# Forgetting attention on one Trainium2 core: unstacked queries and keys, scores as three 64-row products per head, query blocks taken in pairs, probabilities written over their biases

## The chip, the cores and the metric

The kernel runs as one launch on one core of one Trainium2 chip (trn2). The metric is device time in microseconds (us). Lower is better. Of the kernel before there are three runs: 1128.99, 1127.75 and 1128.63 us, median 1128.63 us.

## What is computed

The reference is a two-layer decoder trunk over 512 tokens of width 1024 in float32. Layer 0 is dilated window attention followed by a gated convolutional feed-forward block (FFN). Then keys, values and forget gates are projected once, and layer 1 attends to them with 16 heads of 64 features and runs its own FFN. The change touches only layer 1's attention and the projections that feed it:

```python
def fox_mixer(xn, w_q, w_o, k, v, c):          # c: cumulative log forget gates
    q = (xn @ w_q).reshape(B, T, 16, 64)
    for i in range(T // 128):                   # query blocks of 128
        s = einsum(q[block i], k[:, :q1]) * 64 ** -0.5
        s = s + (c[queries] - c[keys])          # per head
        s = where(causal, s, -1e30)
        p = softmax(s)
        out_i = einsum(p, v[:, :q1])            # keys up to the block's end only
    return concatenate(outs) @ w_o
```

Block i sees (i + 1) * 128 keys, so the four blocks of a head are unequal: 128, 256, 384 and 512 keys.

## The kernel before

**Precision.** The matrix products of the projections and the scores run in the type fp32r, which keeps fewer bits than float32. So every operand is split into a high part (a cast to fp32r) and a low part (value minus high part), and a product becomes three: high times high, high times low, low times high (`mm3`, lines 262 to 265).

**Stages and order.** The kernel has a hand-written order (`manual_schedule`): each engine executes its instructions in the order in which the program issues them, and semaphores hold an instruction back until its operands and its destination buffer are ready. All PSUM tiles come from one pool of 8 banks (`bank`), and the pools of SBUF tiles are `t8` (16 tiles), `t4` (10 tiles) and `t2` (8 tiles). A new tile takes a buffer that an older tile has left, and its first writer waits for that tile's last reader. After layer 0's FFN come the key projections (`keys`, lines 1294 to 1305), the value projections, and the attention loop (lines 1571 to 1607), then the output projection (`po`) and layer 1's FFN.

**Stacked keys and queries.** A head has 64 features, half of the 128 rows of TensorE's array. The kernel stacks the parts: for a head, the key tile `kst` holds the high part in the head's own 64 partitions and the low part in the other 64. The query tile `qst` holds two arrangements, high over low and, swapped, low over high. One product of 128 rows over the first arrangement gives high*high + low*low, and one over the second the two mixed terms, so a head's scores take two products (lines 1493 to 1497). The stacking costs two half-height casts on ScalarE and two half-height subtractions on VectorE for each pair of heads, for keys (1302, 1305) and for queries (`q_high` 1415, `q_low` 1423). The swapped query arrangement is made by two SBUF-to-SBUF DMAs of the GpSimd queue (1425, 1426).

**The loop.** `j` counts 8 pairs of heads, `i` 4 query blocks; a unit is one (j, i) with both heads, 32 units in all. In pass n the program issues, for unit n: `f_scores` (4 products of 128 rows, over at least 256 key columns), the normalisation of unit n-1 (`f_norm`: a reciprocal and two scalings on VectorE), `f_exp` (per head: VectorE adds the bias to the scores in PSUM and takes the row minimum of the negated sum, line 1506; ScalarE takes the exponential with the row sum, 1508), the bias of unit n+1 on GpSimd (`f_bias`, lines 1475 to 1483), a quarter of a later query projection (`q_part`, 6 products of 512 columns), then the transposes of the probabilities of unit n-2 (`f_transpose` on TensorE, 1530, with ScalarE copies out of PSUM, 1532). In every second pass come the products with the values of two older units (`f_pv`, 1545: 64-column products, one head in each half of the array's columns). Around the units, ScalarE and a GpSimd DMA that adds in flight split the weights of a later query projection (`W.high(minus=True)`, lines 54 and 56; `W.low_added`, line 77), SP loads the gates' rows (`load_ck`, 1391) and raw weights, and the finished output is split (`f_out_high` 1555, `f_out_low` 1559). In the last 8 passes the first quarter-products of the output projection (`po.both`) fill in where no query projection is left.

## Time and profile before

| | |
|---|---|
| median of the three runs | 1128.63 us (1127.75 to 1128.99) |
| span of the profiled execution, first to last instruction | 1125.8 us |
| what lies around the span, against the median | 2.83 us |
| TensorE (PE) busy in the span | 1114.3 us, 99% |
| granted TensorE clock, mean | 0.999 of full speed |
| attention loop, first score product to first product of the rest of the output projection | 631.75 to 742.34 us |

The profile gives no other time of the profiled execution than its span, so steps are counted against the span, and 2.83 us are added to compare with runs. A matrix product has two records: its weight load (PEld) and the product (PE). A product's record is longer than the time it holds the array: it includes its way through the array, so the records of consecutive products overlap, and the pace is read from start to start. A tile size like 64*128 in a row is rows by columns of the array that the product uses. A product of float32 operands (not fp32r) appears as two records.

### The profile page before, as it was taken

The page shows a single profiled execution, that of the slowest core. Times are in us where ns is not written, and L with a number is a line of the kernel's source. Part 1 is how long each engine was busy: PE and PEld are TensorE (multiplying, and loading weights), DVE is VectorE, ACT ScalarE, POOL GpSimd, SP SyncE. Part 2 cuts the span into 40 slices and gives each one's busy share as a digit, 9 for nine tenths or more (in the row PEclk, how much of TensorE's full clock was granted, in tenths as well). Part 3 has the DMA queues.
Part 4 walks back from the last instruction along what each step waited for, and adds up shares of the span by engine and source line. Part 5 has one row for each costly group of instructions (what it writes and reads, how often), then busy time and mean ns, then how long its engine had stood idle before and what let it go on. Part 6 is the DMA issues. An engine that isn't in the chain of part 4 may idle for free. (4 is left out here: it accounts for less than half of the span.)

```text
span 1125.8 us, 17268 instructions
## 1 busy us (share of the span) xinstructions
PE 1114.3 (99%) x6267; PEld 950.6 (84%) x6267; DVE 893.8 (79%) x1449; ACT 616.5 (55%) x1038; POOL 191.6 (17%) x291
## 2 busy tenths in 40 slices
PE   9999999999999999999999999999999999999997
PEld 6988889889899888888778888789989989988886
DVE  6668778888888689997588677847888788689894
ACT  5454565545444456576562588746444454456572
POOL 1832101200000121000000556600400000121000
PEclk9999999999999999999999999999999999999999
DMA  9469854333443699793447766473334343499861
GB/s 322 150 222 407 320 161 133 94 119 106 142 123 115 160 346 370 293 333 100 128 151 253 235 168 160 123 209 107 118 94 122 115 138 122 138 351 368 326 243 75
DMA packets 179471, 218.38 MB, mean 194 GB/s; under 512 B 11257, under 2 KB 131049, under 8 KB 179386
## 3 DMA queue, kind: packets, MB, share of 16 engines
q1 hardware_dynamic: 168634, 180.84, 49.0%
q0 software_dynamic: 10752, 36.45, 10.5%
q8 instruction: 49, 0.80, 0.3%
q14 instruction: 36, 0.29, 0.1%
HBM read 166.08 MB, written 39.63 MB: 183 GB/s over the span
## 5 line engine op out<-in xcount | busy, mean ns | idle before, releaser
L592 ACT ACTIVATE bb<-up,conv 128x512 f32<-128x512 f32 x80 | 60.6, 775 | 149.5 <-DVE up L917 76.2
L62 DVE TENSOR_TENSOR w<-wraw,w 128x1024 fp32r<-128x1024 f32 x96 | 123.0, 1312 | 22.1 <-ACT w L54 21.6
L54 ACT CAST w<-wraw 128x1024 fp32r<-128x1024 f32 x110 | 111.6, 1047 | 19.4 <-PE v_ps L264 11.6
L263 PE MATMUL acc<-w 128*128 128x512 f32 (+1 forms) x311 | 120.7, 388 | 1.1 <-DVE mix L310 1.1
L265 PE MATMUL acc<-w 128*128 128x512 f32 (+1 forms) x311 | 120.6, 388 | 0.0
L263 PE MATMUL up<-xch,w 128*128 128x512 f32 (+1 forms) x292 | 104.9, 359 | 0.0
L264 PE MATMUL up<-xcl,w 128*128 128x512 f32 (+1 forms) x292 | 104.9, 359 | 0.0
L263 PE MATMUL up<-xbh,w 128*128 128x512 f32 (+1 forms) x292 | 104.9, 359 | 0.0
L264 PE MATMUL up<-xbl,w 128*128 128x512 f32 (+1 forms) x292 | 104.9, 359 | 0.0
L265 PE MATMUL up<-xbh,w 128*128 128x512 f32 (+1 forms) x292 | 104.8, 359 | 0.0
L265 PE MATMUL up<-xch,w 128*128 128x512 f32 (+1 forms) x292 | 104.8, 359 | 0.0
L264 PE MATMUL acc<-w 128*128 128x512 f32 (+1 forms) x267 | 103.3, 387 | 0.0
L608 POOL DMA_DIRECT2D hD<-hc x42 | 24.2, 576 | 316.9 <-DVE hc L610 316.6
L263 PEld LDWEIGHTS acc<-w 128*128 128x128 f32 x311 | 58.4, 188 | 13.1 <-DVE mix L310 1.3
L265 PEld LDWEIGHTS acc<-w 128*128 128x128 f32 x311 | 58.4, 188 | 12.1 <-DVE w L720 0.3
L593 DVE SCALAR_TENSOR_TENSOR bb<-up,conv,bb 128x511 f32<-128x511 f32 x80 | 59.5, 744 | 7.7 <-ACT bb L592 7.7
L265 PE MATMUL up<-xsh,w 128*128 128x256 f32 x224 | 63.5, 283 | 0.0
L264 PE MATMUL up<-xsl,w 128*128 128x256 f32 x224 | 63.5, 283 | 0.0
L263 PE MATMUL up<-xsh,w 128*128 128x256 f32 x224 | 63.5, 283 | 0.0
L595 DVE SCALAR_TENSOR_TENSOR bb<-up,conv,bb 128x510 f32<-128x510 f32 x80 | 59.9, 749 | 2.8
L263 PEld LDWEIGHTS up<-xbh,w 128*128 128x128 f32 x292 | 55.1, 189 | 8.3
L263 PEld LDWEIGHTS up<-xch,w 128*128 128x128 f32 x292 | 55.1, 189 | 8.2
(303 smaller groups left out, 3040.7 us busy)
## 6 DMA issues: line engine op xcount, KB each, us to landing
wraw<-in_w_up_dram SPq DMA_DIRECT2D x88, 512.0 KB, 4.7
dT<-dsums SPq DMA_DIRECT2D x24, 512.0 KB, 6.5
dsums<-in_w_down_dram SPq DMA_DIRECT2D x22, 512.0 KB, 7.2
dsums<-in_w_down_dram SPq DMA_DIRECT2D x44, 256.0 KB, 6.6
hD<-hc POOLq DMA_DIRECT2D x44, 256.0 KB, 4.7
dact<-hD SPq DMA_DIRECT2D x44, 256.0 KB, 6.2
wraw<-dT SPq DMA_DIRECT2D x22, 512.0 KB, 9.9
wraw<-in_w_down_dram SPq DMA_DIRECT2D x22, 512.0 KB, 6.3
```

Source lines behind the costliest of these rows:

```text
L54: self.nc.scalar.copy(pair[:, 0], raw)
L62: self.nc.vector.tensor_tensor(pair[:, 1], raw, pair[:, 0].bitcast(F32), ALU.subtract)
L263: pe.matmul(o, ah, bh, start=first, stop=False, skip_group_check=shared)
L264: pe.matmul(o, ah, bl, start=False, stop=False, skip_group_check=shared)
L265: pe.matmul(o, al, bh, start=False, stop=last, skip_group_check=shared)
L592: act.activation(bb[:, s, :], ps, AF.Identity, bias=cp[:, 3, ch:ch + 1], scale=cp[:, 2, ch:ch + 1])
L593: dve.scalar_tensor_tensor(bb[:, s, 1:], ps[:, :T - 1], cp[:, 1, ch:ch + 1], bb[:, s, 1:], ALU.mult, ALU.add)
L595: dve.scalar_tensor_tensor(bb[:, s, 2:], ps[:, :T - 2], cp[:, 0, ch:ch + 1], bb[:, s, 2:], ALU.mult, ALU.add)
L608: pool.dma_start(hD[c - 1], hc.pop(c - 1))
```

## The change

- **Keys and queries unstacked.** Two heads stay side by side in the 128 partitions, as the projection leaves them: one full-height cast for the high part, one full-height subtraction for the low part. The swapped query arrangement and its two DMAs for each pair of heads go. A query tile now serves two head pairs.
- **Scores.** A head's scores are three products of 64 rows (high*high, low*high, high*low); the low*low term is no longer computed. The two heads alternate, and write to different PSUM banks.
- **Pairs of blocks.** The loop takes blocks (0, 1) or (2, 3) of a head pair in one pass, 16 pairs and two more passes. The scores of both blocks are issued together, directly followed by the value products of the pair two passes older; then come, for each of the two blocks, bias, query projection quarter, normalisation and transposes of the block of the pass before. Scores of blocks 2 and 3 take four banks at once. The weights' adding DMA moves ahead of the pass's biases, the split that feeds it to the end of the pass before. The fill by the output projection starts at block 26 of 32.
- **Probabilities over biases.** `f_exp` writes into the bias tile; the separate probability tile goes.

```diff
--- before.py
+++ after.py
@@ -27,6 +27,7 @@
 SEVEN = range(6, 19, 2)
 ND = NF // 2
 LAST = 3
+FILL = 26
 
 
 class Weights:
@@ -1286,23 +1287,17 @@
 
     kst = {}
 
-    def halves(hh):
-
-        own = slice(64 * hh, 64 * hh + 64)
-        return own, slice(64 - 64 * hh, 128 - 64 * hh)
+    def key_parts(c):
+        return [kst[c // 2][:, 2 * (c % 2) + i, :] for i in range(2)]
 
     def keys(c):
         o = bank([128, T], name="k_ps")
         feat_mm(W.get(), bd2.xT, o, ALL)
         if c % 2 == 0:
             kst[c // 2] = t8([128, 4, T], F32R, name=f"kst{c // 2}")
-        ts = [kst[(2 * c + hh) // 4][:, (2 * c + hh) % 4, :] for hh in range(2)]
-        for hh in range(2):
-            own, _ = halves(hh)
-            act.copy(ts[hh][own], o[own])
-        for hh in range(2):
-            own, other = halves(hh)
-            dve.tensor_tensor(ts[hh][other], o[own], ts[hh][own].bitcast(F32), ALU.subtract)
+        hi, lo = key_parts(c)
+        act.copy(hi, o)
+        dve.tensor_tensor(lo, o, hi.bitcast(F32), ALU.subtract)
 
     c8 = t2([16, T], name="c8")
 
@@ -1405,25 +1400,21 @@
             bh, bl = xs(xTq, kc, ALL)
             mm3(o, wh[:, kc, :], wl[:, kc, :], bh, bl, kc == 0, kc == KD - 1)
 
+    def query_parts(j):
+        return [qT[j // 2][:, j % 2, i, :] for i in range(2)]
+
     def q_high(j):
         if j >= 8:
             return
-        o = qps[j][0]
-        qT[j] = t = t8([128, 2, 2, T], F32R, name="qst")
-        for hh in range(2):
-            own, _ = halves(hh)
-            act.copy(t[own, 0, hh], o[own])
+        if j % 2 == 0:
+            qT[j // 2] = t8([128, 2, 2, T], F32R, name="qst")
+        act.copy(query_parts(j)[0], qps[j][0])
 
     def q_low(j):
         if j >= 8:
             return
-        o, t = qps.pop(j)[0], qT[j]
-        for hh in range(2):
-            own, other = halves(hh)
-            dve.tensor_tensor(t[other, 0, hh], o[own], t[own, 0, hh].bitcast(F32), ALU.subtract)
-
-        pool.dma_start(t[0:64, 1], t[64:128, 0])
-        pool.dma_start(t[64:128, 1], t[0:64, 0])
+        hi, lo = query_parts(j)
+        dve.tensor_tensor(lo, qps.pop(j)[0], hi.bitcast(F32), ALU.subtract)
 
     cd = tc.dram_tile([16, T], F32, name="cd")
 
@@ -1482,28 +1473,29 @@
                            compare_op=ALU.is_ge, fill=NEG, base=0, channel_multiplier=1)
         bia[j, i] = bias
 
-    def f_scores(j, i):
-        n = (i + 1) * 128
-        nn = max(n, 256)
-        if i < 2:
-            o = bank([128, 2, 256], name="s_ps")
-            s = [o[:, hh] for hh in range(2)]
+    def f_scores(j, i0):
+
+        if i0 == 0:
+            o = [bank([128, 2, 256], name="s_ps") for _ in range(2)]
+            s = [[o[hh][:, i] for hh in range(2)] for i in range(2)]
         else:
-            s = [bank([128, T], name="s_ps") for _ in range(2)]
-        for hh in range(2):
-            hd = 2 * j + hh
-            k = kst[hd // 4][:, hd % 4, :nn]
-            for m in range(2):
-                pe.matmul(s[hh][:, :nn], qT[j][:, m, hh, i * 128:(i + 1) * 128], k, start=m == 0, stop=m == 1)
+            s = [[bank([128, T], name="s_ps") for _ in range(2)] for _ in range(2)]
+        q, k = query_parts(j), key_parts(j)
+        for i in range(2):
+            nn = max((i0 + i + 1) * 128, 256)
+            qs = slice((i0 + i) * 128, (i0 + i + 1) * 128)
+            for n, (a, b) in enumerate(((0, 0), (1, 0), (0, 1))):
+                for hh in range(2):
+                    rows = slice(64 * hh, 64 * hh + 64)
+                    pe.matmul(s[i][hh][:, :nn], q[a][rows, qs], k[b][rows, :nn], start=n == 0, stop=n == 2)
         return s
 
     def f_exp(j, i, s):
         n = (i + 1) * 128
-        bias = bia.pop((j, i))
-        p = t4([128, 2, T], name="prob")
+        p = bia.pop((j, i))
         nm, ls = small(2, "nm"), small(2, "ls")
         for hh in range(2):
-            dve.tensor_tensor_reduce(p[:, hh, :n], s[hh][:, :n], bias[:, hh, :n], -0.125, BIG, ALU.add, ALU.min,
+            dve.tensor_tensor_reduce(p[:, hh, :n], s[hh][:, :n], p[:, hh, :n], -0.125, BIG, ALU.add, ALU.min,
                                      nm[:, hh:hh + 1])
             act.activation(p[:, hh, :n], p[:, hh, :n], AF.Exp, bias=nm[:, hh:hh + 1], scale=-1.0,
                            accum_out=ls[:, hh:hh + 1])
@@ -1558,7 +1550,7 @@
         o, t = ops.pop(j), OTb[j // 2]
         dve.tensor_tensor(t[:, 1, j % 2, :], o, t[:, 0, j % 2, :].bitcast(F32), ALU.subtract)
 
-    units = [(j, i) for j in range(8) for i in range(4)]
+    pairs = [(j, i) for j in range(8) for i in (0, 2)]
     po = Proj(8, 4, lambda kc: (OTb[kc // 2][:, 0, kc % 2, :], OTb[kc // 2][:, 1, kc % 2, :]))
     wo = W.n_get + 7
     fill = [(kc, b) for b in range(2) for kc in range(4)]
@@ -1568,43 +1560,49 @@
         if i == 0:
             W.split(W.n_get + 1)
     f_bias(0, 0)
-    N = len(units)
-    for n in range(N + 3):
-        live = n < N
+    f_bias(0, 1)
+    M = len(pairs)
+    for m in range(M + 2):
+        live = m < M
         if live:
-            j, i = units[n]
-            if i == 0 and j + 1 < 8:
+            j, i0 = pairs[m]
+            if i0 == 0 and j + 1 < 8:
                 load_ck(j + 1)
-            s = f_scores(j, i)
-        if 1 <= n <= N:
-            f_norm(*units[n - 1])
+            s = f_scores(j, i0)
+        if m >= 2:
+            ju, iu = pairs[m - 2]
+            f_pv(ju, iu)
+            f_pv(ju, iu + 1)
         if live:
-            f_exp(j, i, s)
-            if n + 1 < N:
-                f_bias(*units[n + 1])
-            if i == 1:
-                q_low(j + 1)
-            if (j, i) >= (6, 2):
+            for a in range(2):
+                f_exp(j, i0 + a, s[a])
+            if i0 == 2 and j < 6:
+                W.low_added()
+        if m >= 2 and iu == 2:
+            f_out_high(ju)
+        for a in range(2):
+            i = i0 + a
+            if live:
+                if m + 1 < M:
+                    f_bias(pairs[m + 1][0], pairs[m + 1][1] + a)
+                q_part(j + 1 + (i > 0), (i + 3) % 4)
+                if i == 0:
+                    q_high(j + 1)
+                f_norm(j, i)
+            if 1 <= m <= M:
+                f_transpose(pairs[m - 1][0], pairs[m - 1][1] + a)
+            if 0 <= 2 * m + a - FILL < len(fill):
+                po.both(*fill[2 * m + a - FILL])
+            if live and (j, i) >= (6, 2):
                 W.low()
-            elif i == 2:
-                W.low_added()
-            if i == 3 and j:
-                f_out_low(j - 1)
-            q_part(j + 1 + (i > 0), (i + 3) % 4)
-        if 2 <= n < N + 2:
-            f_transpose(*units[n - 2])
-        if n >= N + 3 - len(fill):
-            po.both(*fill[n - N - 3 + len(fill)])
-
-        if n >= 4 and n % 2 == 0:
-            for ju, iu in units[n - 4:n - 2]:
-                f_pv(ju, iu)
-                if iu == 3:
-                    f_out_high(ju)
-        if live and i == 0:
-            q_high(j + 1)
-        if live and (i == 1 if j < 6 else (j, i) >= (6, 1) and W.n_split < wo + 4):
-            W.high(minus=j < 6)
+            if live and (j, i) >= (6, 1) and W.n_split < wo + 4:
+                W.high()
+        if live and i0 == 0:
+            q_low(j + 1)
+            if j < 6:
+                W.high(minus=True)
+        if live and i0 == 2 and j:
+            f_out_low(j - 1)
 
     f_out_low(7)
     W.ahead, W.ahead_dma = 4, 2
```

## The prediction, made before the changed kernel was run

> **What bounds the kernel now.** I read the profile's page first, then the attention loop's stretches, then TensorE's groups, waits and order in time. The page:
>
> ```profile
> span 1125.8 us, 17268 instructions
> PE 1114.3 (99%) x6267; PEld 950.6 (84%) x6267; DVE 893.8 (79%) x1449; ACT 616.5 (55%) x1038; POOL 191.6 (17%) x291
> PEclk9999999999999999999999999999999999999999
> ```
>
> TensorE is the bound, at full clock. What the change takes from other engines is worth nothing unless TensorE waits for it; what it does to TensorE's queue counts in full. The stretches below begin where the scores of block 2 of a head pair begin; the last is the whole loop (length, then busy time of PE, PEld, DVE, ACT, POOL):
>
> ```profile
> core 0: us, PE busy (x) PEld busy (x) DVE busy (x) ACT busy (x) POOL busy (x), PEclk, DMA share, GB/s
> 647.82:661.51 13.69, 13.50 (x103) 11.05 (x102) 10.77 (x32) 11.20 (x29) 8.06 (x15) 1.00 0.73 178
> 661.51:674.73 13.22, 13.22 (x104) 11.13 (x102) 10.50 (x32) 10.74 (x28) 7.98 (x15) 1.00 0.63 160
> 674.73:687.94 13.21, 13.21 (x103) 11.12 (x101) 10.53 (x32) 10.73 (x28) 7.92 (x15) 1.00 0.64 159
> 712.97:726.50 13.53, 12.97 (x99) 10.43 (x98) 12.87 (x33) 11.35 (x28) 11.27 (x16) 1.00 0.46 146
> 631.75:742.34 110.59, 109.37 (x812) 90.08 (x810) 81.70 (x248) 84.17 (x213) 64.52 (x115) 1.00 0.61 163
> ```
>
> A steady head pair takes 13.22 us with TensorE never idle. ACT and DVE have some 2.5 us to spare. The first stretch is 0.47 us longer, and in the fourth DVE is nearly full.
>
> **Term 1, the score products.** Their pace from start to start, in one unit of 256 and one of 384 columns with the projection products around them:
>
> ```profile
> 631.75 0.64 PE L1497 MATMUL s_ps<-kst,qst 128*128 128x256 f32 x4
> 632.22 0.40 PE L263 MATMUL q_ps<-xqh,w 128*128 128x512 f32 x1
> 632.45 0.40 PE L264 MATMUL q_ps<-xql,w 128*128 128x512 f32 x1
> 635.47 0.87 PE L1497 MATMUL s_ps<-kst,qst 128*128 128x384 f32 x4
> 636.17 0.40 PE L263 MATMUL q_ps<-xqh,w 128*128 128x512 f32 x1
> ```
>
> Four products of 256 columns hold the array 0.47 us, four of 384 0.70 us, and 512 columns 0.23 us each, so 0.92 us for four. A head pair has two units of 256, one of 384, one of 512: 2 x 0.47 + 0.70 + 0.92 = 2.56 us, and eight make 20.5 us. After the change a unit has six products, as three pairs of 64 rows. If a pair takes as long as one full product, the scores take 3/4: 15.4 us, **-5.1 us**. If the halves go one after the other, they take 6/4: 30.7 us, **+10.2 us**. Which one? Layer 0's scores are 64-row products too:
>
> ```profile
> L1020 PE MATMUL s_ps<-qkT x32: 272/376/481, 49.2 to 64.1; 64*128 64x256 f32 x24, 64*128 64x128 f32 x8
> L1020 PE MATMUL s_ps<-qkT 64*128 64x256 f32 x8 | 1.1, 388 | 0.0
> ```
>
> Records of 128 columns last 272 ns at the least, those of 256 376 ns in the median. The difference, 104 ns for 128 columns, is their streaming, so 256 columns stream for 0.208 us. Eight of them in a row would take 1.66 us. The second row (a stretch of 1.07 us from 49.72) has all eight in 1.1 us, of which the last record's way through the array, 0.17 us, is no streaming: some 0.95 us. So two row halves do work at once, 1.66 / 0.95 = 1.75 times; the full two is missed because the halves begin half a product apart. These are float32 products, which stream a column in 0.81 ns; the new ones are fp32r at 0.23 us / 512 = 0.45 ns. No row shows 64-row products at that rate, so both ends stay. I take full overlap: the changed code alternates the halves from the first product, with a bank for each.
>
> **Term 2, changes of the array's tile size.** They aren't free:
>
> ```profile
> 48.75 0.49 PE L995 MATMUL qkT_ps<-ident,qk 128*128 128x128 f32 x3
> 49.17 0.39 PE L1020 MATMUL s_ps<-qkT 64*128 64x128 f32 x2
> 643.20 0.49 PE L1530 MATMUL pT_ps<-ident,prob 128*128 128x128 f32 x3
> 643.62 0.33 PE L1545 MATMUL o_ps<-pT,Vt 128*64 128x128 f32 x2
> 644.37 0.28 PE L1545 MATMUL o_ps<-pT,Vt 128*64 128x128 f32 x2
> 644.58 0.39 PE L1497 MATMUL s_ps<-kst,qst 128*128 128x256 f32 x1
> ```
>
> Three transposes start 0.11 us apart (three records of 0.27 make 0.49), so those from 48.75 have streamed by 49.08. The first 64-row product starts at 49.17 and its record is 0.39 instead of 0.27 us: 0.09 + 0.12 = **0.2 us** to enter 64-row mode. From transposes into the value products' column mode: 643.53 to 643.62, and 0.33 for 0.28: **0.15 us**. From the value products (128 columns too, so 0.11) back: 644.48 to 644.58, and 0.39 for 0.28: **0.2 us**. Before, a pair of units pays 0.15 + 0.2 around its value products. After, the order is transposes, scores, value products, projection: 0.2 to enter rows, from rows to columns some 0.15 (not shown; nearest row the entry from transposes; between 0 and 0.2), 0.2 to leave. That is 0.2 us more in each of 16 passes, and the first two passes have no value products, so they leave row mode for 0.2 each: 16 x 0.2 + 2 x 0.2 = **+3.6 us** (between 0.4, if entering cost nothing, and 6.0 if rows to columns cost 0.15 more).
>
> **Term 3, waits that go.** Non-structural delays before:
>
> ```profile
> 640.44 0.36 PE L1497 MATMUL s_ps<-kst,qst 128*128 128x256 f32 x1
> 641.01 0.62 PE L1497 MATMUL s_ps<-kst,qst 128*128 128x256 f32 x3 [0.21 <-DMA qst<-qst]
> 645.39 0.39 PE L264 MATMUL q_ps<-xql,w 128*128 128x512 f32 x1
> 646.00 0.50 PE L265 MATMUL q_ps<-xqh,w 128*128 128x512 f32 x1 [0.22 <-DMA w<-wraw]
> PEld q_ps L265 <- DMA w<-wraw: 1.3, 2, 0.6
> PE o_ps L1545 <- ACT pT L1532: 0.5, 1, 0.5
> ```
>
> The swapped queries came late once: 0.57 us between products that pace 0.12, so 0.45, plus 0.11 of a second weight load, 0.56 us. With no DMA there is nothing left to be late but ScalarE's cast and VectorE's subtraction, and these follow the last quarter of the projection by half a pass. The adding DMA came late twice, 0.61 - 0.23 + 0.11 = 0.49 us the first time and the same again by the stretch that is 13.69 long. It lands 5.9 us after its issue and will be issued ahead of the pass's biases, not behind one:
>
> ```profile
> 640.06 0.93 POOL L77 DMA_DIRECT2D w<-wraw  x1 [0.16 <-issue]
> w<-wraw POOLq DMA_DIRECT2D x6, 512.0 KB, 5.9
> ```
>
> GpSimd then waits for ScalarE's split; behind it stand two biases, which VectorE's first minimum of the next pass needs half a pass later. I count 1.0 us saved, 0 to 1.0. The ScalarE delay in the 712.97 stretch (0.5 us) I keep: weights are still split there. Term 3: **-1.5 us**, bounds 0 and -2.5.
>
> **What costs nothing.** Per head pair these shrink, from two halves to one:
>
> ```profile
> L1302 ACT CAST kst<-k_ps x16: 578/581/583, 556.3 to 600.7; 64x512 fp32r<-64x512 f32 x16
> L1415 ACT CAST qst<-q_ps x16: 580/582/586, 622.4 to 713.1; 64x512 fp32r<-64x512 f32 x16
> L1423 DVE TENSOR_TENSOR qst<-q_ps,qst x16: 683/688/693, 623.6 to 714.4; 64x512 fp32r<-64x512 f32 x16
> L1425 POOL DMA_DIRECT2D qst<-qst x8: 526/557/560, 624.6 to 714.9; - x8
> ```
>
> 16 casts of 0.58 us and 16 subtractions of 0.69 us go, and 16 DMA issues. TensorE's stream hides them all; without that cover ScalarE would gain 9 and VectorE 11 us. Writing probabilities over biases is the same instruction with another destination, but holds each bias buffer until its transposes: six of the ten `t4` tiles, with two gate rows and two raw weights. A late buffer would stop GpSimd, then VectorE; I find each buffer freed half a pass before its need.
>
> **New wait.** Scores of blocks 2 and 3 need four banks. A query projection, an output and the two banks of the transposes just issued are in use; the other four were read by ScalarE and VectorE in the pass before. Behind that group TensorE holds everything. ScalarE decides, by these groups of the stretch 660 to 715 us:
>
> ```profile
> L1532 ACT COPY pT<-pT_ps 128x512 f32<-128x512 f32 x13 | 7.2, 583 | 0.1
> L1508 ACT ACTIVATE prob<-prob,nm 128x256 f32<-128x256 f32 x10 | 5.0, 501 | 0.1
> L56 ACT ACTIVATE w<-wraw 128x1024 fp32r<-128x1024 f32 x4 | 4.3, 1070 | 0.0
> L54 ACT CAST w<-wraw 128x1024 fp32r<-128x1024 f32 x4 | 4.2, 1062 | 0.0
> L1532 ACT COPY pT<-pT_ps 128x384 f32<-128x384 f32 x9 | 3.8, 468 | 0.0
> L1508 ACT ACTIVATE prob<-prob,nm 128x128 f32<-128x128 f32 x8 | 3.1, 394 | 4.3 <-issue 4.3
> ```
>
> Pass lengths on TensorE: with blocks 0 and 1, scores 0.71 + 0.2, value products 6 pairs of 0.11 + 0.15, projection 12 x 0.23, transposes 14 x 0.11, 0.2 to leave: 6.2 us; with blocks 2 and 3 6.7 us; 12.9 together against 13.22. ScalarE in the first: exponentials 2 x 0.39 + 2 x 0.50, query cast 0.58, copies 2 x 0.47 + 2 x 0.58, split 1.06 + 1.07, 6.6 us, of which the copies of the older two banks end a microsecond before the group. So no stop, by a thin margin.
>
> **Sum.** -5.1 + 3.6 - 1.5 = -3.0 us; I allow 0.2 us for small waits: -2.8. Span 1125.8 - 2.8 = 1123.0, and with 2.8 around it **1125.8 us**, against the median 1128.63.
>
> **Rivals.**
> (a) The halves don't overlap at fp32r's rate. Term 1 is then +10.2 and the total 1128.6 + 10.2 + 3.6 - 1.5 = **1140.9 us, slower**. It decides from the point where a pair takes p products' time with 20.5 x (0.75 p - 1) + 3.6 - 1.5 = 0, p = 1.20. For it: the rate is shown for float32 only. Against: overlap itself is plain there.
> (b) They overlap as in the row above, 1.75 times of 2: p = 1.14, scores 17.5 us, term 1 -3.0, total 1128.6 - 3.0 + 3.6 - 1.5 = **1127.7 us**, no difference. For it: the same 64-row forms. Against: the half-product stagger there came from one half's later start. The Trainium skill (TensorE: Matmul & The Clock Gate, Measured speedup vs the span model) lists 3.07 for four row tiles where its own model would give nearly four. As an estimate by that share two tiles would reach 1.54, p = 1.30, on the slower side of (a)'s point, with 1130.2 us. No run here shows fp32r tiles.
> (c) The four-bank group waits for ScalarE's copies (0.58 us each) of the transposes right ahead of it, 0.5 us in 7 of the passes and as much again through VectorE: +3.5 to +7, **1129.3 to 1132.8 us**. For it: ScalarE's 6.6 against 6.2 us. Against: four other banks are free.
> (d) Entering row mode is hidden, since its weights load early: -3.2 more, **1122.6 us**.
>
> **Chances.** Forecast 0.60, (a) 0.12, (b) 0.10, (c) 0.12, (d) 0.06. 0.2% is 2.26 us, about what a measurement of this kernel can tell from no change, so faster means under 1126.4. The forecast's own spread, some 1.2 us by terms 2 and 3, puts 0.45 of its 0.60 there; with (d) faster 0.51. Same: 0.15 + (b) 0.10 + 0.02 of (c) = 0.27. Slower: (a) 0.12 + 0.10 of (c) = 0.22. The range reaches from (d) to (c), 1122.6 to 1132.0, and leaves out (a) and the end of (c).
>
> **What would show it.** Term 1: 64-row records in pairs starting within hundredths of a microsecond, three pairs of 256 columns in 0.36 us; alternate starts 0.12 apart would mean (a). Term 2: 0.2 us ahead of each score group. Term 3: no wait for `qst` or `w` on TensorE. (c): TensorE idle at the 384-column products, released by ScalarE or VectorE. A steady head pair of 12.9 us for 13.22 is the test of the whole. A change of the stages outside the loop would prove me wrong.

## The result, and the profile after

Four runs of the changed kernel took 1122.61 to 1124.48 us, median **1123.84 us**, beside four runs of the kernel before with a median of 1128.81 us (1127.75 to 1131.23). The ratio is 0.9943, with a 95% interval of 0.9925 to 0.9961: about 5.0 us faster, where 2.8 were forecast. The time lies in the range that was given; the gain is 1.8 times the forecast.

The page of the changed kernel:

```profile
span 1122.1 us, 17314 instructions
PE 1111.5 (99%) x6331; PEld 946.1 (84%) x6331; DVE 876.5 (78%) x1433; ACT 606.2 (54%) x1022; POOL 181.1 (16%) x275
PEclk9999999999999999999999999999999999999999
```

TensorE has 64 products more and is busy 2.8 us less. The stretches of the loop, cut as they were for the kernel before (three steady head pairs, the one with the weights' split, the whole loop):

```profile
648.38:661.32 12.94, 12.94 (x110) 10.49 (x110) 8.67 (x30) 10.06 (x27) 7.11 (x13) 1.00 0.46 122
661.32:674.25 12.93, 12.93 (x109) 10.48 (x109) 8.70 (x30) 10.12 (x27) 7.11 (x13) 1.00 0.48 123
674.25:687.19 12.94, 12.94 (x111) 10.49 (x110) 8.69 (x30) 10.13 (x27) 7.12 (x13) 1.00 0.48 123
711.67:724.54 12.87, 12.87 (x110) 10.34 (x109) 11.32 (x33) 11.27 (x28) 6.26 (x10) 1.00 0.26 83
633.22:738.57 105.35, 105.35 (x875) 84.95 (x874) 71.55 (x241) 78.95 (x206) 53.88 (x98) 1.00 0.48 133
```

The loop takes 105.35 us for 110.59, **5.2 us less**, and PE's busy time equals the length in every row: TensorE never stands still. A steady head pair takes 12.93 us, as forecast (12.9). So the surplus does not come from the steady state; it comes from the places where the kernel before was not steady. VectorE is busy 10 us less in the loop, ScalarE 5, GpSimd 11. (Read from the same product as for after, the loop before ends at 742.27, not at 742.34, and is 110.53 us long; the difference to after is 5.2 us either way.)

Behind the loop both kernels take the same time. Ahead of it the profiled execution is 1.5 us later than before (633.22 for 631.75); the last section shows where, in layer 0, which the change leaves alone.

The pace of one pass with blocks 0 and 1 and of one score group with blocks 2 and 3, by the timeline of TensorE (start, length, tile, shape, count):

```profile
634.12 0.50 PE L264 MATMUL q_ps<-xqh,w 128*128 128x512 f32 x1
...
637.11 1.49 PE L1490 MATMUL s_ps<-kst,qst 64*128 64x384 f32 x12
638.53 0.50 PE L264 MATMUL q_ps<-xqh,w 128*128 128x512 f32 x1
...
641.64 0.60 PE L1522 MATMUL pT_ps<-ident,bias 128*128 128x128 f32 x4
642.17 0.98 PE L1490 MATMUL s_ps<-kst,qst 64*128 64x256 f32 x12
643.08 0.88 PE L1537 MATMUL o_ps<-pT,Vt 128*64 128x128 f32 x12
643.88 0.50 PE L264 MATMUL q_ps<-xqh,w 128*128 128x512 f32 x1
644.22 0.39 PE L265 MATMUL q_ps<-xql,w 128*128 128x512 f32 x1
```

Twelve 64-row products of 256 columns go from 642.17 to 643.08, 0.91 us. Issued one behind the other at the 0.118 us of a full product they would need 1.42; as six pairs at 0.118 they need 0.71, and 0.20 is left for entering and leaving row mode (the tile size of 64 rows). The other group: three pairs of 384 columns at 0.175 and three of 512 at 0.23 are 1.22, and 637.11 to 638.53 is 1.42, again 0.20 more. In the records the two halves of a pair start 3 ns apart in most cases. The remaining edges: four transposes at 0.11 are 0.44, but the scores start 0.53 after them (0.09); six pairs of value products at 0.109 are 0.65, and 0.80 pass (0.15, for entering column mode, the tile size of 64 columns, and leaving it); the first projection product takes 0.34 for 0.23 (0.11). A pass pays 0.20 + 0.09 + 0.15 + 0.11 = 0.55 us for changes of tile size; the prediction had 0.2 + 0.15 + 0.2.

Adding up the time from each product's start to the next one's, by kind of product, gives a ledger of the loop without a gap. Its third column is the kernel before with whole casts and without the swapped transfers, from an experiment below:

| us | before | before, second profile | before, relieved | after |
|---|---|---|---|---|
| scores | 24.05 | 25.52 | 23.29 | 18.59 |
| projections | 47.68 | 47.66 | 46.77 | 49.25 |
| transposes | 17.17 | 16.98 | 17.04 | 17.25 |
| value products | 21.25 | 21.25 | 20.25 | 19.89 |
| convolution columns | 0.38 | 0.38 | 0.38 | 0.37 |
| loop | 110.53 | 111.78 | 107.73 | 105.35 |

The value products are the same 320 in all four columns. Undisturbed, 160 pairs at 0.109 and 16 entries and exits at 0.15 are 19.84 us: after has that, before has 1.4 us more, in both profiles. Of that 1.2 us stand in one group, at 714 us: a wait which the prediction meant to keep.

### The profile page after: what moved, and what is told of

Same layout as the page of the kernel before. It is cut to its first block, busy times and chain, and to the rows that moved or that the text cites. A ratio compares the mean times of both kernels' runs of the same rounds, so it can differ in the third digit from the quotient of the medians.

```text
span 1122.1 us, 17314 instructions
## 1 busy us (share of the span) xinstructions
PE 1111.5 (99%) x6331; PEld 946.1 (84%) x6331; DVE 876.5 (78%) x1433; ACT 606.2 (54%) x1022; POOL 181.1 (16%) x275
## 4 chain that ended last, share of the span: by engine, by line
PE 96%; DVE 2%; ACT 1%; issue 0%; DVEq 0%; ACTq 0%
PE up L265 13%; PE up L264 13%; PE up L266 13%; PE acc L264 8%; PE acc L265 8%; PE acc L266 8%; PE v_ps L264 2%; PE v_ps L266 2%; PE v_ps L265 2%; PE qk_ps L264 2%; PE qk_ps L265 2%; PE qk_ps L266 2%; PE o_ps L1537 2%; PE s_ps L1490 2%; PE pT_ps L1522 2%; PE q_ps L264 2%
```

## The experiments

Each is read by the loop's length in its profile, which does not carry what differs outside the loop between executions. Kernel times stand beside it where they were taken in several rounds.

### Does the kernel before repeat?

The same kernel, profiled again.

> The kernel before, profiled a second time: does the loop's length repeat, and do TensorE's waits in it (about 3.4 us by start-to-start times) come at the same places? If they belong to the kernel's order, loop 110.6 us within 0.2 and the same places. If they are chance of one execution (late transfers), the loop differs by up to 1 us and other products wait.

Its loop, and what TensorE waited for in it (line, releaser, total, times, longest):

```profile
633.43:745.21 111.78, 109.05 (x811) 90.01 (x809) 82.00 (x248) 84.19 (x213) 64.26 (x115) 1.00 0.61 162
```

```profile
PE s_ps L1497 <- DMA qst<-qst: 1.7, 2, 1.5
PE o_ps L1545 <- ACT pT L1532: 0.5, 1, 0.5
PE q_ps L265 <- DMA w<-wraw: 0.4, 1, 0.4
```

Neither answer alone: the loop is 1.25 us longer, because the swapped queries were late a second time, by 1.8 us with the product behind the wait, while 0.3 us of small waits at the transposes of 724 to 727 us did not come again. The three late transfers of the first profile (one of swapped queries, two of the split weight) are there again at the same products: 1.3 us in the first profile and 1.4 in the second, product by product against a kernel without the swapped transfers that comes further down. The wait of the value products on ScalarE's copy is there again too, at the same place. So the kernel before has waits that repeat, on three transfers and on ScalarE, and now and then a late transfer that doesn't.

### Order or relief?

What took the waits away: the new order of the loop, or the lighter work of ScalarE, VectorE, GpSimd and the queues? First the two halves of the change, one without the other. The units of before with unstacked 64-row products (with them come the whole casts and subtractions and no swapped transfers, and each unit takes two banks):

```diff
     def f_scores(j, i):
-            for m in range(2):
-                pe.matmul(s[hh][:, :nn], qT[j][:, m, hh, i * 128:(i + 1) * 128], k, start=m == 0, stop=m == 1)
+        for n, (a, b) in enumerate(((0, 0), (1, 0), (0, 1))):
+            for hh in range(2):
+                rows = slice(64 * hh, 64 * hh + 64)
+                pe.matmul(s[hh][:, :nn], q[a][rows, qs], k[b][rows, :nn], start=n == 0, stop=n == 2)
```

> The attention loop took 110.6 us before and 105.35 after. This kernel keeps the loop of before, unit by unit, and takes from the change only the unstacked keys and queries and the 64-row products. Both theories: scores 3 streams for 4, -5.1; but row mode is entered and left in every unit, 0.4 us in 16 units and 0.2 in the other 16, +9.6; no transfer of swapped queries, -0.6. Theory (the order by pairs took the waits on ScalarE and VectorE away, about 1.9 us): they stay here, loop 114.5 us, kernel 1132.7. Rival (the smaller casts and subtractions took them away): they go here too, loop 112.6, kernel 1130.8.

And the pairs of after with stacked 128-row products, halved casts and subtractions, and the swapped transfers:

```diff
     def f_scores(j, i0):
-            for n, (a, b) in enumerate(((0, 0), (1, 0), (0, 1))):
-                for hh in range(2):
-                    rows = slice(64 * hh, 64 * hh + 64)
-                    pe.matmul(s[i][hh][:, :nn], q[a][rows, qs], k[b][rows, :nn], start=n == 0, stop=n == 2)
+            for hh in range(2):
+                for m in range(2):
+                    pe.matmul(s[i][hh][:, :nn], qT[j][:, m, hh, qs], k, start=m == 0, stop=m == 1)
```

> The loop of after, in pairs and with probabilities over biases, but keys and queries stacked and four products of 128 rows as before, with the halves' casts and subtractions and the swapped-query transfers. No row mode, so neither the 5.1 us of the scores nor the 3.5 us of mode changes. Theory (the order took all waits away, 3.3 to 3.5 us): no stall on TensorE, loop 107.2 us, kernel 1125.4. Rival (the relief of the other engines and the missing transfer took the larger part away): the waits on ScalarE, VectorE and the swapped queries stay, and only the adding transfer's 0.9 go, loop 109.7, kernel 1127.9.

The loops of the first and the second:

```profile
631.32:743.93 112.61, 112.10 (x875) 85.27 (x875) 74.62 (x241) 79.66 (x206) 52.33 (x98) 1.00 0.45 127
```

```profile
633.74:746.16 112.42, 109.89 (x811) 91.08 (x810) 76.73 (x248) 83.96 (x213) 63.08 (x115) 0.98 0.63 162
```

The units in rows came to 112.61 us, the rival's number: 110.53 - 5.1 + 9.6 is 115.0, so 2.4 us of waits are gone without any new order. The kernel took 1129.84 us (ratio 1.0009, 1.0000 to 1.0019): the new products in the old order are worth nothing, because row mode is entered and left twice as often: by start-to-start times scores and transposes take 22.47 and 20.02 us here (0.6 of it one wait), 18.59 and 17.25 in after. The pairs with stacked products met neither expectation: 112.42 us, 1132.08 us (ratio 1.0034, 1.0020 to 1.0049), a little slower than before. The new order subtracts the queries at the end of a pass, so the first swapped transfer of the loop is issued 6.1 us after the loop's start, where before has 5.0, and TensorE waits for it:

```profile
642.73 0.36 PE L1500 MATMUL s_ps<-kst,qst 128*128 128x256 f32 x1
645.19 1.55 PE L1500 MATMUL s_ps<-kst,qst 128*128 128x256 f32 x7 [2.09 <-DMA qst<-qst]
```

My theory, that the order took all waits away, falls: alone it makes a worse one. For the wait of the value products it holds, though: the 28 products that take 2.89 us in before take 1.68 here, undisturbed, with the casts and subtractions still in halves. And without its waits the row kernel's stream was also 4.5 us longer than before's (9.6 of mode changes less 5.1 of scores), which gives the other engines time. To part this, the old work was given back to both row kernels: casts and subtractions in halves, a query tile for each head pair, transfers that nobody reads.

```diff
     def q_high(j):
-        act.copy(query_parts(j)[0], qps[j][0])
+        for hh in range(2):
+            own = slice(64 * hh, 64 * hh + 64)
+            act.copy(query_parts(j)[0][own], qps[j][0][own])
     def q_low(j):
-        dve.tensor_tensor(lo, qps.pop(j)[0], hi.bitcast(F32), ALU.subtract)
+        for hh in range(2):
+            own = slice(64 * hh, 64 * hh + 64)
+            dve.tensor_tensor(lo[own], o[own], hi[own].bitcast(F32), ALU.subtract)
+        pool.dma_start(t[0:64, 1], t[64:128, 0])
+        pool.dma_start(t[64:128, 1], t[0:64, 0])
```

> The units in 64-row products of the first experiment (loop 112.6 us, one wait of some 0.9 us left of 3.4), with the old work of the other engines given back: queries cast and subtracted in two halves of 64 rows, a tile of its own for each head pair, and both swapped-query transfers issued by GpSimd; nobody reads what they bring. The scores do not wait for the transfers. Theory 1 (the relief took the waits of before away): about 2 us of waits come back, loop 114.5. Theory 2 (TensorE's own mode changes, 2 us longer over the loop, gave the other engines time): loop stays at 112.6.

> After, in pairs and with 64-row products, and the same old work given back: queries cast and subtracted in halves, a tile for each head pair, swapped-query transfers that nobody reads. Theory 1 (relief decides, the order does not): 1.5 to 2 us of waits on ScalarE, VectorE and the adding transfer come back, loop 107. Theory 3 (the order by pairs has slack enough for the old work): no wait, loop 105.4.

The loops, units and pairs:

```profile
633.45:747.02 113.57, 112.53 (x875) 85.36 (x875) 76.85 (x248) 84.07 (x213) 63.66 (x114) 1.00 0.60 158
```

```profile
633.40:740.74 107.34, 106.43 (x875) 85.00 (x874) 77.93 (x248) 84.06 (x213) 65.33 (x114) 1.00 0.65 167
```

In units 1.0 us comes back, between the two theories; in pairs 2.0 us, as theory 1 said. The order by pairs does not absorb the old work as a whole. But the waits stand at other places: the 28 value products take 1.68 us in pairs and 1.82 in units, for 2.89 in before. What TensorE waits for in the second kernel is a weight's low part, the adding transfer, and ScalarE's copies in the first head pair:

```profile
PE acc L265 <- DVE w L63: 0.4, 1, 0.4
PE q_ps L266 <- DMA w<-wraw: 0.3, 1, 0.3
PE o_ps L1543 <- ACT pT L1530: 0.2, 1, 0.2
```

### The relief alone, on the kernel before

The cleanest test leaves order and products as before and only lightens the queries: one cast and one subtraction of full height, first with the transfers, then without. Both kernels compute other scores (the parts lie in other rows), in the same instructions on TensorE.

```diff
     def q_high(j):
-        for hh in range(2):
-            own, _ = halves(hh)
-            act.copy(t[own, 0, hh], o[own])
+        act.copy(t[:, 0, 0], o)
     def q_low(j):
-        for hh in range(2):
-            own, other = halves(hh)
-            dve.tensor_tensor(t[other, 0, hh], o[own], t[own, 0, hh].bitcast(F32), ALU.subtract)
+        dve.tensor_tensor(t[:, 0, 1], o, t[:, 0, 0].bitcast(F32), ALU.subtract)
```

> Before, stacked products in units, but the queries cast and subtracted whole, by one instruction each instead of two; the transfers stay. The two heads' queries and their low parts then lie in the wrong rows for the stacked products, so the scores computed are others; TensorE's instructions are the same. Before's loop was 110.53 us and 111.78 in a second profile, of which waits on late transfers 1.4 and 2.4, on ScalarE and VectorE some 2.0 and 1.8. Theory (fuller ScalarE and VectorE make those waits): about 1.1 us or more of them go, loop 109.4 to 110.0, and the wait of the value products (0.87 us with its successors) is gone or halved. Rival (that wait comes from the order of the units): loop 110.5 or more, the wait as before.

> The same without the swapped-query transfers: the second product of each head reads the first one's operand again, so the scores are others still, in the same instructions on TensorE. Theory (the relief of the other engines and queues is all of term 3): no wait left, loop 110.53 - 3.4 = 107.1 us. Rival (row mode's longer passes or the order by pairs had a share): waits on ScalarE or VectorE stay, loop 108 to 110.

Their loops, and the value products at the fixed wait, in the kernel before, in the first, in the second, and in after:

```profile
631.94:740.71 108.77, 108.05 (x812) 90.11 (x810) 70.05 (x241) 79.71 (x206) 62.94 (x112) 1.00 0.63 166
```

```profile
631.96:739.70 107.74, 107.74 (x812) 90.01 (x810) 72.61 (x241) 79.64 (x206) 54.31 (x98) 1.00 0.47 132
```

```profile
714.06 0.88 PE L1545 MATMUL o_ps<-pT,Vt 128*64 128x128 f32 x12
715.44 1.57 PE L1545 MATMUL o_ps<-pT,Vt 128*64 128x128 f32 x16 [0.51 <-ACT pT L1532]
```

```profile
713.04 2.08 PE L1541 MATMUL o_ps<-pT,Vt 128*64 128x128 f32 x28
```

```profile
712.76 2.12 PE L1538 MATMUL o_ps<-pT,Vt 128*64 128x128 f32 x28
```

```profile
713.09 1.75 PE L1537 MATMUL o_ps<-pT,Vt 128*64 128x128 f32 x28
```

Whole casts and subtractions alone bring the loop to 108.77 us, 1.8 less than before, more than expected; without the transfers it is 107.74, **2.8 us less with nothing changed on TensorE**. Product by product, of the 1.8 us 1.0 is value products, 0.3 transposes and 0.3 transfers (two waits less, one of 0.8 us more); of the 2.8, value products 1.0, transposes 0.3 and late transfers 1.4. The 28 value products of the split's head pair should take 28 / 2 x 0.109 + 0.15 = 1.68 us. From their records, before takes 2.89 (1.21 too many, the same in the second profile to 0.02), the relieved kernels 2.01 and 2.05, after 1.68. So in the old order whole casts and subtractions take 0.9 of the 1.2 us away. They are not the only thing that does: in the pairs all of it is gone, with halves too, and in the units in rows as well (1.68 us). In after several causes, each nearly enough alone, lie on top of each other. The row's 0.51 showed less than half of the wait in before: the products behind it started late without a gap of their own. The waits of the weight loads (PEld), read for these products alone, show 1.0 us in two waits for ScalarE's copies.

VectorE gained more than the subtractions. In the first of these kernels it is busy 11.7 us less in the loop, of which the subtractions are 4.8; the rest are the scalings of the probabilities (L1518, 35.2 us in all before, 28.0 here). One of 256 columns takes 0.35 us alone, but in before 7 of the 16 ran beside a bias of GpSimd and took 0.79 to 1.88; in the first relieved kernel none takes longer than 0.36. It is a matter of when the two meet: with the halves given back to the units in rows none does either. One of the seven, and the bias beside it:

```profile
702.32 1.88 DVE L1518 TENSOR_SCALAR prob<-prob,rl 128x256 f32<-128x256 f32 x1
702.69 1.36 POOL L1480 TENSOR_SCALAR bias<-ck,cq 128x512 f32<-128x512 f32 x2
```

What of TensorE's waits is due to these meetings, and what to the halves themselves, was not separated.

### Which engine?

After again, with one piece of the old work at a time (the edits of the diff above, each alone).

> After, with one part of the old work given back: queries cast by ScalarE and subtracted by VectorE in two halves of 64 rows; no transfers. With halves and transfers together the loop was 107.34 us, 2.0 longer than after's 105.35. If the waits come from ScalarE and VectorE being fuller (1.3 us each per head pair), most of it is here: loop 106.5 to 107.3. If they come from GpSimd and the DMA queues, nothing: 105.4.

> After, with the other part of the old work given back: a query tile for each head pair and both swapped-query transfers issued by GpSimd, which nobody reads; casts and subtractions whole, as after. If GpSimd and the DMA queues make the waits: loop 106.5 to 107.3, among them the adding transfer's (0.45 us in the first head pair). If ScalarE and VectorE make them: 105.4, or 105.8 with the adding transfer's alone.

> After, with only ScalarE's cast of the queries in two halves. Both halved together gave 106.44 us against 105.35. If ScalarE is the narrow engine (0.58 us more per head pair) most of the 1.09 us is here: 106.2; if VectorE is, 105.4.

> After, with only VectorE's subtraction of the queries in two halves (0.69 us more per head pair). If VectorE is the narrow engine: loop 106.2 us, with the output projection's product waiting for a weight's low part (0.41 us); if ScalarE is, 105.4.

Both halves, transfers, ScalarE's halves, VectorE's halves:

```profile
633.40:739.84 106.44, 106.10 (x875) 85.03 (x874) 77.06 (x248) 83.93 (x213) 55.53 (x100) 1.00 0.47 132
```

```profile
633.30:738.74 105.44, 105.44 (x876) 84.91 (x875) 72.13 (x241) 79.07 (x206) 61.71 (x112) 1.00 0.65 169
```

```profile
631.87:737.86 105.99, 105.84 (x876) 85.04 (x875) 72.23 (x241) 83.75 (x213) 54.96 (x99) 1.00 0.48 133
```

```profile
633.43:738.98 105.55, 105.54 (x875) 84.91 (x875) 76.41 (x248) 78.95 (x206) 54.72 (x99) 1.00 0.49 133
```

Against 105.35: +1.09, +0.09, +0.64, +0.20, one profile each; four loops without any of the casts and subtractions given back (after, this one with transfers, and two experiments below) lie between 105.30 and 105.44. ScalarE's work is the dearer: 4.8 us more on it cost 0.6, 4.9 more on VectorE 0.2. These costs are few single waits: 0.41 of ScalarE's 0.64 stands at one product of the output projection, VectorE's 0.20 at one value product of the first head pair. Transfers that nobody reads cost nothing by themselves. The pieces don't add: alone they make 0.9, together 2.0, so what the lighter work buys depends on all of it being light.

### Was the earlier issue of the adding transfer worth something?

The prediction gave it 1.0 us. Forward in the kernel before, and back again in the kernel after:

```diff
 # before, moved ahead
+            if i == 2 and j < 6:
+                W.low_added()
             if n + 1 < N:
                 f_bias(*units[n + 1])
-            elif i == 2:
-                W.low_added()
```

```diff
 # after, moved back
-            if i0 == 2 and j < 6:
-                W.low_added()
                 f_norm(j, i)
+                if i == 2 and j < 6:
+                    W.low_added()
```

> Before, with one move: the adding weight transfer is issued by GpSimd ahead of the next unit's bias instead of behind it. Theory (it was late because it stood behind the bias): both waits of 0.49 us go, loop 110.6 - 1.0 = 109.6. Rival (it is late because of the swapped-query transfers and ScalarE's split ahead of it): no change, 110.6.

> After, with one move undone: the adding weight transfer is issued behind a bias again, not ahead of both. The prediction gave this move 1.0 us. If it was the move: two waits of 0.49 us come back, loop 106.3. If it was the relief (the units in 64-row products had no such wait with the transfer behind the bias): loop 105.4.

```profile
634.08:749.73 115.65, 110.09 (x811) 89.84 (x810) 82.37 (x248) 83.61 (x213) 65.02 (x115) 1.00 0.60 157
```

```profile
631.82:737.12 105.30, 105.30 (x875) 84.96 (x874) 74.88 (x241) 78.93 (x206) 54.51 (x98) 1.00 0.48 133
```

It was not the move. In after, undoing it changes nothing. In before it costs 4 to 5 us against its two profiles, which neither theory had. GpSimd's own timeline has it stand at the transfer's issue for ScalarE's split, with the bias behind it:

```profile
640.91 0.91 POOL L77 DMA_DIRECT2D w<-wraw  x1 [0.65 <-ACT w L56]
641.55 1.67 POOL L1480 TENSOR_SCALAR bias<-ck,cq 128x512 f32<-128x512 f32 x2
```

TensorE's list in that kernel has longer waits of both kinds:

```profile
PE o_ps L1545 <- ACT pT L1532: 3.3, 5, 1.5
PE q_ps L265 <- DMA w<-wraw: 1.2, 1, 1.2
```

Why the transfer, issued earlier, was waited for longer (1.2 us for 0.4) stays open. For the value products, between which and the bias stand VectorE's minimum and ScalarE's exponential, the trace has two candidates. In the pass at 683 us the bias is ready at 685.55 and the minimum starts at 685.69; and the two scalings just ahead of that minimum, beside the same bias, took VectorE 1.89 us, where before has 0.90. Neither was tried by itself. The waits on the adding transfer are gone in the units in rows, in after and in the relieved kernel without transfers, whichever way its issue stands; with the swapped transfers 0.3 us of them was left.

### Do the row halves need to alternate, and are fewer mode changes worth it?

```diff
-            for n, (a, b) in enumerate(((0, 0), (1, 0), (0, 1))):
-                for hh in range(2):
+            for hh in range(2):
+                for n, (a, b) in enumerate(((0, 0), (1, 0), (0, 1))):
```

> After, with the three products of head 0 issued ahead of the three of head 1 instead of alternating. If each row half runs its own queue, head 1 starts with head 0's first product and the loop stays at 105.35 us. If products start in issue order and only neighbours overlap, the two at the seam alone lie side by side: 5 streams for 3, scores 25.7 for 15.4 us, loop 115.6.

```profile
634.12:739.56 105.44, 105.44 (x876) 85.12 (x875) 71.63 (x241) 78.93 (x206) 53.85 (x98) 1.00 0.48 133
```

No: three products of one head and then three of the other take as long. They still start as three pairs, 10 ns apart in most cases instead of 3, so the fourth product issued starts ahead of the second: each row half takes its products from the stream on its own, three ahead at least. Then the value products of four blocks together, in every second pass:

```diff
-            f_pv(ju, iu)
-            f_pv(ju, iu + 1)
+            if iu == 2:
+                for i in range(4):
+                    f_pv(ju, i)
```

> After, with the value products of all four blocks of a head pair together in every second pass, so that rows to columns is paid 8 times less. The passes without them go from rows straight to the projection and pay the leaving price as they do now. Theory (each entry to column mode costs 0.15 us, and nothing else limits): loop 105.35 - 8 x 0.15 = 104.15 us, kernel 1122.6. Rival (the transposed probabilities now wait in their buffers a pass longer, and ScalarE's copies stand behind them): TensorE stalls at the transposes, loop 105.4 or more.

```profile
631.33:736.27 104.94, 104.33 (x876) 85.23 (x875) 72.55 (x241) 78.23 (x206) 53.87 (x98) 1.00 0.48 132
```

```profile
719.50 0.48 PE L264 MATMUL acc<-w,OTb 128*128 128x512 f32 x1
720.58 0.50 PE L265 MATMUL acc<-w,OTb 128*128 128x512 f32 x1 [0.61 <-DVE w L63]
```

0.4 us of the 1.2 (the kernel took 1123.15 us, 1121.80 to 1123.98, ratio 0.9948, 0.9933 to 0.9963), because a shorter pass brings an output projection product to a weight whose low part VectorE hasn't made. With that fill half a pass later (`FILL = 27`):

> After with the value products of four blocks together, as in the fourth experiment (loop 104.94 us, where one output projection product waited 0.77 us for VectorE's low part of a weight), and the output projection's fill one half pass later, so that the weight is there. If that wait was all that stood in the way: loop 104.94 - 0.77 = 104.2, kernel 1122.4. Rival (the fill now runs out of cover at the end of the loop): 104.9 or more, 1123.1.

```profile
631.46:735.78 104.32, 104.32 (x876) 85.34 (x875) 73.41 (x242) 79.80 (x208) 53.89 (x98) 1.00 0.50 137
```

104.32 us and no wait: 1.0 us less than after. The kernel's time is 1122.06 us (1121.33 to 1123.55), ratio 0.9939 (0.9925 to 0.9953); by times it can't be told from after's 0.9943, by the loop it is ahead.

## Why the prediction was half right

- **Term 1, scores, -5.1 us: right.** Two row halves of fp32r overlap fully. Rivals (a) and (b) are out. The Trainium skill (TensorE: Matmul & The Clock Gate, Measured speedup vs the span model) would by its share, as an estimate, have led to 1130.2 us; here two tiles reach 2.0 of 2: behind the entry, pairs of 256 columns start 0.116 to 0.120 us apart, as full products do.
- **Term 2, mode changes, +3.6 us: right.** 0.55 us a pass measured, against 0.35 in a pair of units before: 16 x 0.20, and 0.25 at the loop's two ends, +3.45. Rows to columns was the one without a row; 0.15 was near enough. Rival (d) is out.
- **Term 3, waits that go, -1.5 us: this is the step that failed.** The kind was right, the size was not: 110.53 - 5.1 + 3.45 leaves 108.9, the loop took 105.35, so 3.5 us of waits went. The transfers' 1.5 us went about as forecast (1.4). Of the missing 2.0 us 1.4 were late value products (1.2 of them in the group that waited for ScalarE's copies), 0.3 transposes that were late in this one profile, and 0.3 are not located. Two sentences of the prediction carry the error. "The ScalarE delay in the 712.97 stretch (0.5 us) I keep: weights are still split there" took 0.5 us from the products' list of waits (for the split weight the prediction had used that of the weight loads) where the records hold 1.2, and kept it because the split stayed; but the casts of the same stretch went (0.9 of the 1.2 us in the old order), and the order by pairs alone would have taken all of it. And under what costs nothing, "TensorE's stream hides them all" was said of the casts and subtractions for the whole loop, from steady stretches in which it is true. Given back to the kernel after, the query halves cost it 1.1 us; taken from the kernel before, together with the transfers, they saved it 2.8.
- **The 0.2 us for small waits** did not come; TensorE waits for nothing in the loop. Rival (c) is out: no score group of four banks was held up.
- The 1.0 us for the adding transfer was luck: its waits did go, but not by the reason given (issued ahead of a bias). The move is worth nothing in after, and a loss in before.
- **What stays open:** 107.74 - 5.13 + 3.45 is 106.06, and after took 105.35. Of these 0.7 us, 0.35 is the remainder of the value products' wait, which the pairs take away and the units in rows too; the rest is not located. Which of the pairs' parts (later values, normalisation in its own pass, probabilities over biases) does it wasn't tried.

## What to carry to other kernels

An engine that is busy for three quarters of a loop (ScalarE 84 of 111 us, VectorE 82) is no free engine: work taken from it is worth what TensorE waits for it in the fullest stretch, and that is counted from start-to-start times against the undisturbed pace, not from the products' listed waits alone, which showed less than half of the largest one (the weight loads' list showed most of it). Profile a kernel twice before pricing its late transfers: here three repeated and one did not. When several parts of a change could each have removed a wait, look for that wait in every experiment: the one of the value products went with lighter casts and with the new order alike. And products in two row halves, three for four stacked ones, pay only where the order lets many of them share one change of the array's tile size: the same products in units of one block gained nothing.

## What the runs showed of the hardware

- Six products in two row halves start in pairs whether they are issued alternately (3 ns apart, loop 105.35 us) or three and three (10 ns apart, 105.44).
- A scaling on VectorE is slower while GpSimd computes a bias beside it: with 256 columns it took 0.35 us alone and up to 1.88 so.
- A stall can be followed by a slower clock. In the pairs with stacked products, TensorE stood 2.09 us for the swapped queries, and behind it the granted clock was 0.56 for 3.5 us, some 1.5 us more:

```profile
645.19:648.70 3.51, 3.51 (x20) 2.90 (x21) 1.92 (x11) 1.86 (x8) 3.35 (x6) 0.56 0.35 72
```

  Stalls of 1.53 us in the second profile of before and in before with the adding transfer ahead were not followed by that. The Trainium skill (TensorE: Matmul & The Clock Gate, Part 1: The HAM clock gate) puts the fall behind an idle window of about 3.4 us; the runs differ, and they decide: here the clock fell behind stalls of 2.09 us and, as the next point shows, 1.24 us.
- The same stall can be followed by a fall in one execution and not in the next. This is where the profiled execution of after lost its 1.5 us ahead of the loop. In all 18 profiles TensorE waits 1.24 us for VectorE at a score product of layer 0; in after:

```profile
121.11 1.30 PE L1023 MATMUL s_ps<-qkT 64*128 64x128 f32 x8 [1.24 <-DVE qkT L999]
```

  The clock behind it, first in the kernel before, then in after:

```profile
122.00:128.00 6.00, 6.00 (x31) 4.99 (x30) 5.21 (x19) 4.54 (x18) 0.00 (x0) 1.00 1.01 394
```

```profile
122.00:128.00 6.00, 6.00 (x24) 4.87 (x23) 5.24 (x19) 4.55 (x18) 0.00 (x0) 0.72 1.01 390
```

  6.0 x 0.28 is 1.7 us. In ten of the 18 profiles the clock fell to one half for 3.4 us, beginning 0.8 to 2.1 us after the end of that stall; in eight it did not. It belongs to the execution and not to the kernel: the loops of the ten start at 633.2 to 634.1 us and those of the eight at 631.3 to 632.0, and before is among both. What tells them apart in the traces is when the stall begins, counted from the moment at which the clock first became full, 8 to 12 us into the span: 109.3 to 110.6 us after it in the ten, 109.0 or less and 111.0 or more in the eight. The gain of the loop, 5.2 us, is free of this; kernel times hold it by chance.
- The time around the span is 1.8 to 2.2 us in the runs whose span is known, not the 2.83 that the prediction took from a median and another run's span.
